# Strassen block products in the down projection of a transformer layer, with sums kept in DRAM

## The chip, the cores and the metric

The kernel runs on one core of a Trainium2 chip. The metric is the device time of one launch in microseconds. The kernel before was timed three times: 3572.49, 3582.17 and 3583.19, median 3582.17. All data is float32. A core has TensorE (PE in the profile; its weight loads PEld), VectorE (DVE), ScalarE (ACT), GpSimd (POOL) and SyncE (SP), which here issues all of the DMAs, one after another.

## The reference

One transformer layer on 2048 tokens of width 1024: modulated norm, an input projection, attention beside a gated linear recurrence, an output projection, and then the feed-forward part, where the change is.

```python
def swiglu(h, w_gu, w_down):
    a, b = jnp.split(h @ w_gu, 2, axis=-1)
    return (jax.nn.silu(a) * b) @ w_down
...
x = x + mx[2] * (jnp.concatenate([att_x, hg_x], axis=-1) @ w_out[l])
x = x + mx[5] * swiglu(modulate(rmsnorm(x, g_norm2[l]), mx[3], mx[4]), w_gu[l], w_down[l])
...
return rmsnorm(x, g_final)
```

`w_gu` is 1024x5632, `w_down` 2816x1024; 2816 is 22 blocks of 128.

## The kernel before

Every large product takes each float32 operand as a high part (rounded to the type fp32r) and a low part (what is left), and adds three matmuls: high by high, high by low, low by high. A converted tile so costs one ACT copy (the high part) and one subtraction on DVE or POOL (the low part).

**Stages.** Modulation vectors; input projection; attention and recurrence, interleaved; output projection in blocks of four token tiles of 128 (`project_token`, `mix_token`, `normed_block`, blocks 0 to 3 in turn); then the feed-forward part in two passes over halves of the tokens, pass 1 (tokens 1024 to 2047) first, then pass 0. The normed rows of blocks 2 and 3 stay in SBUF for pass 1; those of blocks 0 and 1 go through DRAM (`s_h2`).

**A pass** has three functions. `build(pair)` makes the sums T1 to T4 of the four blocks of the transposed input (DVE at L1092) and their parts (L999, L1000). `hidden(pair)` computes gate and up by Strassen's seven block products (Winograd's form): for each of the 22 blocks `ff` it loads 2 x 512 KB of `w_gu` (L1128), forms the sums S1 to S4 on POOL (L1141) and their parts (L1135, L1136), and runs seven products of 12 matmuls each (L1161) into PSUM banks A, B and C, copied and combined through tiles `r` (L1173 to L1189), giving `h` (L1189, L1195), stored to `s_hid`. `down(pair)` is a plain product: for each half `hb` of the pass's tokens, over 22 blocks `ff`, it loads 256 KB of `s_hid` (L1216) and 512 KB of `w_down` (L1218), converts both (L1221, L1222, L1225, L1226), and adds 24 matmuls (L1230) into all eight PSUM banks. After the last `ff` of a half, each of the four token tiles is finished: gate multiply (L1244), reload of the row `x1` into a single buffer (L1239) and add (L1245), squares on ACT (L1247), norm (L1249, L116, and the power on POOL at L118), scale (L1252), store (L1254). The next half's matmuls need the banks which L1244 empties.

**What sets the order.** In these stages a scheduler orders the instructions of each engine from its own estimate of the times; within a stage the tiles' buffer counts (`dw` 2, `hid` 3, `wraw` 2 for each of two tags, `tmp` 8) decide how far loads and conversions run ahead. `build(0)` is stepped through inside `down(1)` (`next(side, 0)`, every second `ff`).

Of the kernel before, what the change touches and what calls it, by code (L numbers as in the profile page):

```python
# [48 lines left out]

C_Q, C_K, C_HQ, C_I, C_FF, C_FB, C_G = 0, 512, 768, 1280, 1792, 2304, 2816  # L50
# [17 lines left out]
def block_kernel(ctx: ExitStack, tc: tile.TileContext, a: dict, out: bass.AP, dbg=None):  # L68
# [28 lines left out]
    s_hid = [dram(f"s_hid{j}", [NFF, P, 1024]) for j in range(2)]  # L97
# [468 lines left out]
    with ExitStack() as st:  # L566
# [333 lines left out]
        for item in work + [None]:  # L900
            if item is None:
# [51 lines left out]
                mix_token(0)  # L953
# [26 lines left out]
    with ExitStack() as st:  # L980
        np5 = pool(p5, "np5", 6)
        ep = pool(p5, "ep", 2)
# [22 lines left out]
        def project_token(t):  # L1005
# [7 lines left out]
            for hf in range(2):  # L1013
# [8 lines left out]
                if hf == 0 and t + 1 < NCH:  # L1022
                    mix_token(t + 1)
# [7 lines left out]
        def normed_block(blk, xns):  # L1031

            tb = blk % 2
            for k in range(KT):
# [4 lines left out]
                x = slot(vA, F32)  # L1039
# [14 lines left out]
        for blk in range(4):  # L1054
# [14 lines left out]
        tmp = pool(st, "tmp", 8, side="right")  # L1069
        wraw = pool(st, "wraw", 2, side="right")  # L1070
        hraw = pool(st, "hraw", 4, side="right")
# [42 lines left out]
        def hidden(pair):  # L1114


            with ExitStack() as d1:
# [48 lines left out]
                nxt = weights(0)  # L1166
                for ff in range(NFF):
                    nm = f"{pair}_{ff}"
                    W = nxt
                    A, B, C = (bank(f"p{n}{nm}") for n in "ABC")  # L1170
                    product(A, W["A11"], V["B11"], True, False)
                    r0 = t512(f"r0{nm}")
                    nc.scalar.activation(r0, A, AF.Copy)  # L1173
# [11 lines left out]
                    product(C, W["A12"], V["B21"], True, True)  # L1185
                    nc.vector.tensor_tensor(r0, C, r0, op=ALU.add)
                    nc.scalar.activation(r0, r0, AF.Silu)
                    h1 = t512(f"h1{nm}")
                    nc.gpsimd.tensor_tensor(h1, r1, r4, op=ALU.mult)  # L1189
                    nc.sync.dma_start(s_hid[pair][ff][:, 512:], h1)  # L1190
                    if ff + 1 < NFF:
                        nxt = weights(ff + 1)
                    product(A, W["A22"], V["T4"], False, True)
                    h0 = t512(f"h0{nm}")
                    nc.vector.tensor_tensor(h0, A, r0, op=ALU.mult)  # L1195
                    nc.sync.dma_start(s_hid[pair][ff][:, :512], h0)

        def down(pair, side):

            with ExitStack() as d2:  # L1200

                dw = pool(d2, "dw", 2)
                hid = pool(d2, "hid", 3)
                yp = pool(d2, "yp", 2)
# [6 lines left out]
                for hb in range(2):  # L1211
                    acc = [[bank(f"pd{pair}{hb}{j}{hf}") for hf in range(2)] for j in range(4)]
                    for ff in range(NFF):
# [19 lines left out]
                        if ff % 2:  # L1233
                            next(side, 0)
# [25 lines left out]
        down(1, todo)  # L1260
        for _ in todo:
            pass
        hidden(0)
        down(0, iter(()))


# [41 lines left out]
```

## Time and profile before

| | |
|---|---|
| median of three runs | 3582.17 us |
| profiled execution, its own time | 3583.7 us |
| its span (first to last instruction) | 3581.9 us, so 1.8 us lie outside |
| PE busy in the span | 3352.1 us (94 %) |
| DVE, ACT, POOL busy | 1757.0, 1549.5, 1593.0 us |
| moved by DMA | 355.97 MB, 99 GB/s in the mean |
| output projection's last matmuls | at 2114 us |
| `hidden(1)`, `down(1)` | about 2127 to 2584, 2585 to 2842 us |
| `hidden(0)`, `down(0)` | about 2866 to 3303, 3303 to 3558 us |

PE is the engine that is busy nearly all of the time, so the time is read as PE's work at the spacing of its matmuls, plus the stretches in which it idles or runs at a lower granted clock. "Idle" in a row of the trace stands in brackets, with the instruction that ended it.

### The profile page before, as it was taken

To read this page: it belongs to the slowest core of one execution; us is meant where nothing else is said; L and a number is where in the kernel's file an instruction comes from. 1 tells how busy PE (TensorE), PEld (TensorE's weight loads), DVE (VectorE), ACT (ScalarE), POOL (GpSimd) and SP (SyncE) were. 2 spreads that over 40 slices of the span, in tenths; PEclk is the share of its full clock that TensorE was granted. 3 is DMA by queue.
4 is the path that set the end of the run, shared out by engine and by line. 5 is a ranking of instruction groups with operands and counts; after the bars stand their busy time and mean duration, and the time that the engine had idled before them with its cause. 6 is when DMAs were issued, how large, how long until landed. Compare 5 with 4: busy or idle time off the path is not lost. (4 is left out here: it accounts for less than half of the span.)

```text
span 3581.9 us, 52481 instructions
## 1 busy us (share of the span) xinstructions
PE 3352.1 (94%) x19588; PEld 2793.6 (78%) x19588; DVE 1757.0 (49%) x3078; ACT 1549.5 (43%) x3167; POOL 1593.0 (44%) x1496
## 2 busy tenths in 40 slices
PE   8999999979999899999999988999999799999997
PEld 5999877968777778777777876888787678887876
DVE  6445555066667677666655474222354332222344
ACT  4322222157767567766654133333433233333232
POOL 4322232068768758768742046555201165553010
PEclk9999999989999999999999999999999899999998
DMA  7244655321121121111005432222445322222553
GB/s 231 95 140 123 176 167 167 109 85 32 36 63 34 33 69 44 31 46 40 23 24 162 159 106 74 91 76 83 150 146 171 121 92 89 73 88 85 162 173 104
DMA packets 315696, 355.97 MB, mean 99 GB/s; under 512 B 27088, under 2 KB 245168, under 8 KB 315184
## 3 DMA queue, kind: packets, MB, share of 16 engines
q1 hardware_dynamic: 315440, 352.61, 31.7%
q8 instruction: 154, 2.52, 0.3%
q14 instruction: 102, 0.84, 0.1%
HBM read 251.85 MB, written 100.68 MB: 98 GB/s over the span
## 5 line engine op out<-in xcount | busy, mean ns | idle before, releaser
L827 POOL TENSOR_TENSOR pr<-pr,fac 128x768 f32<-128x768 f32 x256 | 374.4, 1484 | 215.0 <-DMA mf<-in_k_mask_dram 101.5
L815 DVE TENSOR_REDUCE neg<-s 128x1 f32<-128x768 f32 x384 | 365.1, 954 | 199.0 <-PE s L812 198.4
L812 PE MATMUL s<-K,qs 128*128 128x512 f32 (+1 forms) x1536 | 371.5, 364 | 33.7 <-ACT pr L820 31.6
L820 ACT ACTIVATE pr<-s,neg 128x768 f32<-128x768 f32 x384 | 348.5, 908 | 73.6 <-DVE neg L819 38.1
L812 PEld LDWEIGHTS s<-K,qs 128*128 128x128 f32 x1536 | 264.0, 191 | 104.8 <-ACT pr L820 44.9
L835 PE MATMUL pt<-identr,pr 128*128 128x128 f32 x2304 | 319.8, 274 | 7.6 <-DVE oo L870 3.2
L841 ACT ACTIVATE pf<-pt 128x512 f32<-128x512 f32 x448 | 256.7, 601 | 111.4 <-PE pt L835 109.5
L1230 PE MATMUL pd<-dl,hh 128*128 128x512 f32 x704 | 277.8, 395 | 2.7 <-DVE dl L1226 2.7
L1230 PE MATMUL pd<-dh,hl 128*128 128x512 f32 x704 | 277.4, 394 | 0.0
L835 PEld LDWEIGHTS pt<-identr,pr 128*128 128x128 f32 x2304 | 261.3, 141 | 16.6 <-ACT pf L841 7.5
L848 PE MATMUL av<-pf,V 128*64 128x256 f32 x2304 | 268.7, 388 | 1.5 <-DVE pf L839 1.5
L848 PEld LDWEIGHTS av<-pf,V 128*64 128x64 f32 x2304 | 162.4, 139 | 88.3 <-issue 9.7
L1230 PE MATMUL pd<-dh,hh 128*128 128x512 f32 x704 | 181.7, 394 | 17.9 <-DVE yy L1244 14.4
L1245 POOL TENSOR_TENSOR yy<-yy,xf 128x512 f32<-128x512 f32 x24 | 30.6, 1296 | 364.6 <-DVE yy L1244 348.7
L1221 ACT ACTIVATE hh<-hr 128x512 fp32r<-128x512 f32 x88 | 55.4, 630 | 292.2 <-PE pd L1230 289.4
L1222 DVE TENSOR_TENSOR hl<-hr,hh 128x512 fp32r<-128x512 f32 x88 | 61.7, 701 | 231.7 <-ACT hh L1221 229.8
L1230 PEld LDWEIGHTS pd<-dh,hh 128*128 128x128 f32 x704 | 133.6, 190 | 48.8 <-DVE yy L1244 16.2
L635 PE MATMUL pa<-Q,M 128*128 128x128 f32 x896 | 131.4, 291 | 30.7 <-POOL Q L661 16.8
L1230 PEld LDWEIGHTS pd<-dl,hh 128*128 128x128 f32 x704 | 134.3, 191 | 31.7 <-DVE dl L1226 3.6
L1230 PEld LDWEIGHTS pd<-dh,hl 128*128 128x128 f32 x704 | 134.3, 191 | 28.2
L635 PEld LDWEIGHTS pa<-Q,M 128*128 128x128 f32 x896 | 116.4, 195 | 38.7 <-POOL Q L661 20.5
L1161 PE MATMUL pA<-x,A11h 128*128 128x512 f32 x352 | 118.9, 403 | 23.9 <-ACT A11h L1135 23.9
(290 smaller groups left out, 8698.8 us busy)
## 6 DMA issues: line engine op xcount, KB each, us to landing
w<-in_w_gu_dram SPq DMA_DIRECT2D x88, 512.0 KB
wr<-in_w_down_dram SPq DMA_DIRECT2D x88, 512.0 KB
wm<-in_w_mod_dram SPq DMA_DIRECT2D x24, 1024.0 KB
s_hid<-h SPq DMA_DIRECT2D x88, 256.0 KB
hr<-s_hid SPq DMA_DIRECT2D x88, 256.0 KB
s_q<-sq SPq DMA_DIRECT2D x128, 128.0 KB
qs<-s_q SPq DMA_DIRECT2D x32, 512.0 KB
ws<-in_w_in_dram SPq DMA_DIRECT2D x9, 1024.0 KB
```

Of the source, the lines that this page charges most:

```text
L635: nc.tensor.matmul(pa[:, cs], M[:, cs], strided(Q[:], c * P, [[2 * hs, 64 // hs], [512 + hs, 2], [1, hs]]), start=True, stop=True)
L812: nc.tensor.matmul(s[:, o:o + w], self.qs[:, hh, self.item[2], half, :], self.kv[0][:, k0 + o:k0 + o + w], start=(half == 0), stop=(half = ...
L815: nc.vector.tensor_reduce(neg[:, i:i + 1], s[:, :n], axis=AX.X, op=ALU.min)
L820: nc.scalar.activation(pr[:, k0:k0 + n], s[:, :n], AF.Exp, bias=neg[:, m:m + 1], scale=-1.0, accum_out=self.ls[:, hh, i:i + 1])
L827: nc.gpsimd.tensor_tensor(pj, pj, self.fac[:, hh, j:j + 1].to_broadcast([P, SW]), op=ALU.mult)
L835: nc.tensor.transpose(pt[:, (2 * i + hh) * P:(2 * i + hh + 1) * P], self.prs[hh][:, (2 * k2 + i) * P:(2 * k2 + i + 1) * P], ident)
L841: nc.scalar.activation(pf, pt, AF.Copy)
L848: nc.tensor.matmul(self.av[i * 64:(i + 1) * 64], self.kv[1][:, 2 * k2 + i, :], self.pf[k2][:, i * 256:(i + 1) * 256], start=(n == 0), stop ...
L1161: nc.tensor.matmul(acc, w[wi][:, k, :], x[xi][k], start=(start and k == 0 and i == 0), stop=(stop and k == KH - 1 and i == 2), skip_group_ ...
L1221: nc.scalar.activation(hh, hr, AF.Copy)
L1222: nc.vector.tensor_tensor(hl, hr, f32v(hh), op=ALU.subtract)
L1230: nc.tensor.matmul(acc[j][hf], l[:, j * P:(j + 1) * P], r[:, hf * 512:(hf + 1) * 512], start=(ff == 0 and i == 0), stop=(ff == NFF - 1 and ...
```

## The change

The down projection becomes a Strassen product too. The pass's 8 token tiles, `w_down`'s 22 rows of blocks and its 1024 columns are each cut in two, and seven block products take the place of the plain one. Each has 11 steps (`NHF`), a step having 4 token tiles x 3 matmuls: 132 matmuls a product, 924 a pass (1056 before).

- The left operands (A11, A12, A22 and the sums S1 to S4 of the hidden values) are made in `hidden`, on POOL, and stored to DRAM by their names: seven stores of 256 KB for two blocks `ff` (four before). For that `hidden` takes blocks j and j+11 in turns.
- The right operands' sums T1 to T4 of `w_down` are made once, beside `hidden(1)` (`right_sums`): 44 loads of 256 KB, 44 DVE subtractions, 44 stores to DRAM (`s_wt`). Both passes read them.
- `down` loads two times 256 KB for each step, converts each half with one ACT copy and one DVE subtraction (128x512), in two sets of tiles (`dwa`, `dwb`) used in turns.
- The eight rows tiles `y` of a pass are loaded once at its start and kept; each product's result is multiplied by the gate (DVE) and added to its rows (POOL, DVE for the last product) at the product's end. Norm and stores follow for four tiles at the sixth product's end, for the other four at the seventh's. The last two steps of the seventh product are taken token by token.
- In `hidden`, `first(ff)` draws the loading, the sums and the product A11 of the next block ahead, and the product with B21 is now the second. `tmp` has 10 buffers; `hraw` is gone.
- The output projection takes blocks 2, 3, 0, 1 in this order, so that pass 1's rows are made first. Rows of blocks 0 and 1 go through the pool `ep` on their way to DRAM (3 buffers), `np5` has 5.

```diff
-                x = slot(vA, F32)
+                x = slot(vA if blk >= 2 else ep, F32)
...
-        for blk in range(4):
+        for blk in (2, 3, 0, 1):
...
-        tmp = pool(st, "tmp", 8, side="right")
+        tmp = pool(st, "tmp", 10, side="right")
         wraw = pool(st, "wraw", 2, side="right")
-        hraw = pool(st, "hraw", 4, side="right")
...
+                def first(ff):
+                    W = weights(ff)
+                    A = bank(f"pA{pair}_{ff}")
+                    product(A, W["A11"], V["B11"], True, False)
+                    r0 = t512(f"r0{pair}_{ff}")
+                    nc.scalar.activation(r0, A, AF.Copy)
+                    return W, A, r0
+
+                def store(n, j, t):
+                    nc.sync.dma_start(s_hid[pair][n][j], t)
...
+                order = [j + half * NHF for j in range(NHF) for half in range(2)]
+                with tc.high_priority():
+                    nxt = first(order[0])
+                h = {}
+                for n, ff in enumerate(order):
+                    half, j = divmod(ff, NHF)
+                    W, A, r0 = nxt
+                    B, C = (bank(f"p{b}{nm}") for b in "BC")
+                    product(C, W["A12"], V["B21"], True, True)
+                    nc.vector.tensor_tensor(r0, C, r0, op=ALU.add)
+                    nc.scalar.activation(r0, r0, AF.Silu)
...
+                    nc.gpsimd.tensor_tensor(r1, r1, r4, op=ALU.mult)
+                    if n + 1 < NFF:
+                        nxt = first(order[n + 1])
                     product(A, W["A22"], V["T4"], False, True)
-                    h0 = t512(f"h0{nm}")
-                    nc.vector.tensor_tensor(h0, A, r0, op=ALU.mult)
-                    nc.sync.dma_start(s_hid[pair][ff][:, :512], h0)
+                    nc.vector.tensor_tensor(r0, A, r0, op=ALU.mult)
+                    h[half] = r0, r1
+                    store(("A11", "A12")[half], j, r0)
+                    if half:
+                        store("A22", j, r1)
+                        (a11, a21), (a12, a22) = h[0], h[1]
+                        s3, s2, s4 = (t512(f"s{i}{nm}") for i in "324")
+                        nc.gpsimd.tensor_tensor(s3, a11, a21, op=ALU.subtract)
+                        store("S3", j, s3)
+                        nc.gpsimd.tensor_tensor(a21, a21, a22, op=ALU.add)
+                        store("S1", j, a21)
+                        nc.gpsimd.tensor_tensor(s2, a21, a11, op=ALU.subtract)
+                        store("S2", j, s2)
+                        nc.gpsimd.tensor_tensor(s4, a12, s2, op=ALU.subtract)
+                        store("S4", j, s4)
+                        h = {}
+                        next(side, 0)
...
+        def right_sums():
+            for j in range(NHF):
+                b = {}
+                for r in range(2):
+                    for c in range(2):
+                        t = b[r, c] = tmp.tile([P, 512], F32, tag="x", name=f"wq{j}{r}{c}")
+                        nc.sync.dma_start(t, quadrant(r, c, j))
+                nc.vector.tensor_tensor(b[0, 0], b[0, 1], b[0, 0], op=ALU.subtract)
+                nc.sync.dma_start(s_wt["T1"][j], b[0, 0])
+                nc.vector.tensor_tensor(b[0, 1], b[1, 1], b[0, 1], op=ALU.subtract)
+                nc.sync.dma_start(s_wt["T3"][j], b[0, 1])
+                nc.vector.tensor_tensor(b[1, 1], b[1, 1], b[0, 0], op=ALU.subtract)
+                nc.sync.dma_start(s_wt["T2"][j], b[1, 1])
+                nc.vector.tensor_tensor(b[1, 0], b[1, 0], b[1, 1], op=ALU.subtract)
+                nc.sync.dma_start(s_wt["T4"][j], b[1, 0])
+                yield
...
         def down(pair, side):
+                dwa = pool(d2, "dwa", 4)
+                y0p = pool(d2, "y0p", 4)
+                dwb = pool(d2, "dwb", 4)
+                y1p = pool(d2, "y1p", 4)
...
+                direct = {"B11": (0, 0), "B21": (1, 0), "B22": (1, 1)}
+                step = [0]
+                def load(ln, rn, j):
+                    n = step[0]
+                    step[0] += 1
+                    raw = wraw.tile([P, D], F32, tag=f"w{n % 2}", name=f"lr{pair}_{n}")
+                    nc.sync.dma_start(raw[:, :512], s_hid[pair][ln][j])
+                    nc.sync.dma_start(raw[:, 512:], quadrant(*direct[rn], j) if rn in direct else s_wt[rn][j])
+                    out = []
+                    for i in range(2):
+                        src = raw[:, i * 512:(i + 1) * 512]
+                        hi, lo = ((dwa, dwb)[n % 2].tile([P, 512], F32R, tag="p", name=f"{x}{pair}_{n}{i}")
+                                  for x in ("dh", "dl"))
+                        nc.scalar.activation(hi, src, AF.Copy)
+                        nc.vector.tensor_tensor(lo, src, f32v(hi), op=ALU.subtract)
+                        out.append((hi, lo))
+                    return out
...
+                def add(acc, tb, cb, t, eng):
+                    cs = slice(cb * 512, (cb + 1) * 512)
+                    x = tmp.tile([P, 512], F32, tag="x", name=f"yg{pair}{tb}{cb}{t}_{step[0]}")
+                    nc.vector.tensor_tensor(x, acc, gate2[:, cs], op=ALU.mult)
+                    eng.tensor_tensor(ys[tb, t][:, cs], ys[tb, t][:, cs], x, op=ALU.add)
...
+                plan = [("A11", "B11", "A", 1, 0, (0, 0)), ("S1", "T1", "B", 1, 0, (1, 1)),
+                        ("S2", "T2", "A", 0, 0, (0, 1)), ("S4", "B22", "B", 0, 1, (0, 1)),
+                        ("S3", "T3", "A", 0, 0, (1, 1)), ("A12", "B21", "C", 1, 1, (0, 0)),
+                        ("A22", "T4", "A", 0, 1, (1, 0))]
+                for n, (ln, rn, bk, start, stop, (tb, cb)) in enumerate(plan):
...
+                    def mms(t, j, f):
+                        (lh, ll), (rh, rl) = f
+                        for i, (l, r) in enumerate(((lh, rh), (lh, rl), (ll, rh))):
+                            nc.tensor.matmul(cur[t], l[:, t * P:(t + 1) * P], r,
+                                             start=bool(start and j == 0 and i == 0),
+                                             stop=bool(stop and j == NHF - 1 and i == 2), skip_group_check=True)
+                    kept = []
+                    for j in range(NHF):
+                        f = load(ln, rn, j)
+                        if n == 0 and j == 1:
+                            rows(0)
+                            rows(1)
+                        if last and j >= NHF - 2:
+                            kept.append((j, f))
+                            continue
+                        for t in range(4):
+                            mms(t, j, f)
+                        if step[0] % 7 == 0:
                             next(side, 0)
+                    for t in range(4):
+                        for j, f in kept:
+                            mms(t, j, f)
+                        add(cur[t], tb, cb, t, nc.vector if last else nc.gpsimd)
+                        if n == 3 or n == 5:
+                            square(0, 1 if n == 3 else 0, t)
+                        if n == 4:
+                            square(1, 1, t)
+                            nc.gpsimd.tensor_tensor(ys[1, t][:, 512:], ys[1, t][:, 512:], gfin[:, 512:], op=ALU.mult)
+                        if n == 5:
+                            rs = norm(0, t)
+                            nc.vector.scalar_tensor_tensor(ys[0, t], ys[0, t], rs, gfin, op0=ALU.mult, op1=ALU.mult)
+                            nc.sync.dma_start(out[0, row(0, t), :], ys[0, t])
+                        if n == 6:
+                            square(1, 0, t)
+                            rs = norm(1, t)
+                            y = ys[1, t]
+                            nc.vector.scalar_tensor_tensor(y[:, :512], y[:, :512], rs, gfin[:, :512],
                                                            op0=ALU.mult, op1=ALU.mult)
+                            nc.scalar.activation(y[:, 512:], y[:, 512:], AF.Copy, scale=rs)
+                            nc.sync.dma_start(out[0, row(1, t), :], y)
...
-        hidden(1)
+        hidden(1, right_sums())
         todo = build(0)
         down(1, todo)
         for _ in todo:
             pass
-        hidden(0)
+        hidden(0, iter(()))
         down(0, iter(()))
```

PE executes 1848 matmuls of the down projection instead of 2112; the number of those of `hidden` (3696) and of all stages before is as it was. Three places show what moved.

First SP's queue, where `hidden(0)` ends and `down(0)` begins. Before (`hr`, `wr` are the loads of `down`, `xf` the first row that is reloaded, the numbers behind them the step):

```order
1087 L1218 DMA wr_3_31403<-in_w_down_dram 128x1024
1088 L1196 DMA s_hid_86<-h_19_31013 128x512
1089 L1190 DMA s_hid_86<-h_20_31102 128x512
1090 L1196 DMA s_hid_86<-h_20_31157 128x512
1091 L1190 DMA s_hid_86<-h_21_31246 128x512
1092 L1208 DMA gate_31281<-s_mod 128x1024
1093 L1210 DMA gfin_31283<-in_g_final_dram 128x1024
1094 L1196 DMA s_hid_86<-h_21_31261 128x512
1095 L1239 DMA xf_32085<-s_x_83 128x1024
1096 L1216 DMA hr_4_31437<-s_hid_86 128x512
```

And now (`lr` is the load of a step, `y` the rows kept):

```order
1317 L1179 DMA s_hid0A_87<-r_21_31718 128x512
1318 L1179 DMA s_hid0S_90<-s_21_31822 128x512
1319 L1289 DMA y_31893<-s_x_83 128x1024
1320 L1289 DMA y_31895<-s_x_83 128x1024
1321 L1179 DMA s_hid0S_92<-s_21_31823 128x512
1322 L1289 DMA y_31897<-s_x_83 128x1024
1323 L1289 DMA y_31899<-s_x_83 128x1024
1324 L1289 DMA y_31901<-s_x_83 128x1024
1325 L1289 DMA y_31903<-s_x_83 128x1024
1326 L1289 DMA y_31905<-s_x_83 128x1024
1327 L1271 DMA lr_5_31988<-s_hid0A_86 128x512
1328 L1272 DMA lr_5_31988<-in_w_down_dram 128x512
```

The load of step 4 stood behind the last store and one row's load; now step 5's stands behind the last stores and all eight rows' loads, and step 6's, not shown, just ahead of this piece.

Next DVE at the end of `down(0)`. Before, the last two token tiles (`yy` is the row tile, `pd` the PSUM bank):

```order
2806 L1244 TENSOR_TENSOR yy_32997<-pd_32163,gate_31281 128x512
2807 L1244 TENSOR_TENSOR yy_32997<-pd_32164,gate_31281 128x512
2808 L1252 SCALAR_TENSOR_TENSOR yy_32979<-yy_32979,rs_xf_32991,gfin_31283 128x1024
2809 L1245 TENSOR_TENSOR yy_32997<-yy_32997,xf_32995 128x512 x2
2810 L1249 TENSOR_TENSOR ss1f_33005<-ssf_32998 128x1
2811 L116 TENSOR_SCALAR ms_xf_33007<-ss1f_33005 128x1
2812 L1244 TENSOR_TENSOR yy_33015<-pd_32165,gate_31281 128x512
2813 L1244 TENSOR_TENSOR yy_33015<-pd_32166,gate_31281 128x512
2814 L1252 SCALAR_TENSOR_TENSOR yy_32997<-yy_32997,rs_xf_33009,gfin_31283 128x1024
2815 L1245 TENSOR_TENSOR yy_33015<-yy_33015,xf_33013 128x512 x2
2816 L1249 TENSOR_TENSOR ss1f_33023<-ssf_33016 128x1
```

And now, the last three (`y` the row tile, `yg` the bank times the gate):

```order
3007 L1310 TENSOR_TENSOR ss1f_33799<-ssf_33212 128x1
3008 L1297 TENSOR_TENSOR y_31903<-y_31903,yg_77_33814 128x512
3009 L121 TENSOR_SCALAR ms_xf_33801<-ss1f_33799 128x1
3010 L1296 TENSOR_TENSOR yg_77_33834<-pd0A_31856,gate_31849 128x512
3011 L1365 SCALAR_TENSOR_TENSOR y_31901<-y_31901,rs_xf_33803,gfin_31851 128x512
3012 L1310 TENSOR_TENSOR ss1f_33819<-ssf_33219 128x1
3013 L1297 TENSOR_TENSOR y_31905<-y_31905,yg_77_33834 128x512
3014 L121 TENSOR_SCALAR ms_xf_33821<-ss1f_33819 128x1
3015 L1365 SCALAR_TENSOR_TENSOR y_31903<-y_31903,rs_xf_33823,gfin_31851 128x512
3016 L1310 TENSOR_TENSOR ss1f_33839<-ssf_33226 128x1
3017 L121 TENSOR_SCALAR ms_xf_33841<-ss1f_33839 128x1
3018 L1365 SCALAR_TENSOR_TENSOR y_31905<-y_31905,rs_xf_33843,gfin_31851 128x512
```

Multiply, add, norm and scale of the four tiles are now woven into each other, with no load of a row among them, and each tile has half a row (512 columns) here: the first half of the columns of these four tiles is the last to be ready, the other half has its multiply by `gfin` from POOL after the fifth product and its scale by the norm from ACT.

Last DVE inside `down(1)`, where the second product has ended, at step 22. Before, a stretch with as much of `build(0)` in it (L1092, the sums):

```order
2346 L1092 TENSOR_TENSOR x_26521<-x_26257,x_26241 128x512
2347 L1092 TENSOR_TENSOR x_26523<-x_26259,x_26243 128x512
2348 L1092 TENSOR_TENSOR x_26525<-x_26261,x_26245 128x512
2349 L1092 TENSOR_TENSOR x_26527<-x_26263,x_26247 128x512
2350 L1222 TENSOR_TENSOR hl_0_26174<-hr_0_26169,hh_0_26173 128x512
2351 L1226 TENSOR_TENSOR dl_0_26178<-wr_0_26171,dh_0_26177 128x1024
2352 L1092 TENSOR_TENSOR x_26617<-x_26265,x_26521 128x512
2353 L1222 TENSOR_TENSOR hl_1_26210<-hr_1_26205,hh_1_26209 128x512
```

And now (L1096 is the same line of `build`, `dl` the low parts of a step):

```order
2435 L1279 TENSOR_TENSOR dl_220_27038<-lr_22_27034,dh_220_27037 128x512
2436 L1279 TENSOR_TENSOR dl_221_27042<-lr_22_27034,dh_221_27041 128x512
2437 L1296 TENSOR_TENSOR yg_22_27022<-pd1B_26733,gate_26412 128x512
2438 L1296 TENSOR_TENSOR yg_22_27025<-pd1B_26734,gate_26412 128x512
2439 L1296 TENSOR_TENSOR yg_22_27028<-pd1B_26735,gate_26412 128x512
2440 L1296 TENSOR_TENSOR yg_22_27031<-pd1B_26736,gate_26412 128x512
2441 L1096 TENSOR_TENSOR x_27172<-x_26613,x_26597 128x512
2442 L1096 TENSOR_TENSOR x_27174<-x_26615,x_26599 128x512
2443 L1096 TENSOR_TENSOR x_27176<-x_26617,x_26601 128x512
2444 L1096 TENSOR_TENSOR x_27178<-x_26619,x_26603 128x512
2445 L1279 TENSOR_TENSOR dl_230_27061<-lr_23_27057,dh_230_27060 128x512
2446 L1279 TENSOR_TENSOR dl_231_27065<-lr_23_27057,dh_231_27064 128x512
```

Between the low parts of step 22 and those of step 23 there are now eight operations in a row, four at the product's end and four of `build(0)`.

105 lines of the change are left out of this document (37 added, 68 removed).

## The prediction

> **What bounds the kernel.** I read the busy totals first, then the matmul groups of the down projection, then PE's timeline for its spacing and idle gaps, then windows around the gaps, last the chain of waits at the end.
>
> ```profile
> PE 3352.1 (94%) x19588; PEld 2793.6 (78%) x19588; DVE 1757.0 (49%) x3078; ACT 1549.5 (43%) x3167; POOL 1593.0 (44%) x1496
> L1230 PE MATMUL pd<-dl,hh 128*128 128x512 f32 x704 | 277.8, 395 | 2.7 <-DVE dl L1226 2.7
> L1230 PE MATMUL pd<-dh,hl 128*128 128x512 f32 x704 | 277.4, 394 | 0.0
> L1230 PE MATMUL pd<-dh,hh 128*128 128x512 f32 x704 | 181.7, 394 | 17.9 <-DVE yy L1244 14.4
> ...
> 3462.37 0.39 PE L1230 MATMUL pd<-dh,hl 128*128 128x512 f32 x1
> ...
> 3463.73 0.39 PE L1230 MATMUL pd<-dh,hl 128*128 128x512 f32 x1
> ...
> 3450.00:3550.00 100.00, 100.00 (x443) 82.80 (x442) 38.25 (x42) 29.91 (x40) 0.55 (x1) 1.00 0.43 134
> 2400.00:2500.00 100.00, 100.00 (x429) 80.39 (x428) 27.19 (x43) 36.04 (x63) 53.30 (x40) 1.00 0.27 85
> ```
>
> PE is busy 94 % of the span. The down projection has 3 x 704 = 2112 matmuls. A single one takes 0.39 us, but they overlap, so the mean of a group is no price: the two rows of the timeline are six starts apart, (3463.73 - 3462.37)/6 = 0.2267 us each. The window of `down` agrees: 100/0.2267 = 441, and 443 are in it with those cut at its edges. The window of the hidden products, by the same two fewer, gives 100/427 = 0.2342, say 0.2343. What is left beside this work are gaps. Windows give, in this order: length, busy us and count of PE, PEld, DVE, ACT, POOL, then the granted clock, the DMA share and GB/s.
>
> ```profile
> 2719.92 0.79 PE L1230 MATMUL pd<-dh,hh 128*128 128x512 f32 x1 [5.14 <-DVE yy L1244]
> 2700.00:2740.00 40.00, 31.45 (x122) 24.71 (x121) 20.31 (x32) 13.14 (x26) 12.76 (x12) 0.87 0.55 179
> 3430.00:3460.00 30.00, 21.86 (x80) 16.80 (x79) 14.76 (x21) 8.75 (x18) 9.21 (x10) 0.89 0.63 214
> 2575.00:2605.00 30.00, 25.55 (x102) 19.79 (x101) 24.34 (x37) 18.31 (x30) 1.29 (x1) 0.94 0.49 165
> 3295.00:3325.00 30.00, 28.46 (x123) 22.70 (x122) 11.10 (x14) 9.95 (x14) 1.29 (x1) 1.00 0.54 193
> 2841.49 0.39 PE L1230 MATMUL pd<-dh,hl 128*128 128x512 f32 x1
> 2865.76 1.22 PE L1161 MATMUL pA<-x,A11h 128*128 128x512 f32 x2 [23.88 <-ACT A11h L1135]
> 2161.22 1.22 PE L1161 MATMUL pA<-x,S2h 128*128 128x512 f32 x2 [12.10 <-ACT r L1173]
> 3558.02 0.39 PE L1230 MATMUL pd<-dh,hl 128*128 128x512 f32 x1
> 3570.33 3.50 DMA xf<-s_x
> ```
>
> A gap costs its idle time and the lower clock behind it, so I take a window less its matmuls at full spacing. The changes of token half lose 40 - 122 x 0.2267 = 12.3 us in pass 1 and 30 - 80 x 0.2267 = 11.9 in pass 0; entering `down` loses 30 - 102 x 0.2267 = 6.9 and 30 - 123 x 0.23 = 1.7. From `down(1)` to `hidden(0)` PE idles 23.9 us, and behind the last matmul (3558.4) the span goes on for 23.5 us, of which each token waits 3.5 us for its row's reload.
>
> **The change, part by part**, against the profiled execution (3583.7 us, of which 1.8 lie outside the span; the median of the runs shown is 1.5 lower).
>
> *1. Fewer matmuls.* 2112 - 1848 = 264 fewer at 0.2267: **-59.8**. Should the new operands run at the hidden products' 0.2343, each of 1848 costs 0.0076 more, +14.0. I keep 0.2267: the converted tiles of both operands again lie in `down`'s own pools.
>
> *2. Change of token half.* It goes: **-24.2**. What comes in its place is term 7.
>
> *3. Tail.* The rows are in SBUF. These are the durations of the last 28 us:
>
> ```profile
> L1245 DVE TENSOR_TENSOR yy<-yy,xf 128x512 f32<-128x512 f32 x8 | 5.2, 686 | 2.9 <-DMA xf<-s_x 2.9
> L1247 ACT ACTIVATE xf<-yy 128x512 f32<-128x512 f32 x8 | 5.0, 624 | 22.3 <-DVE yy L1245 22.3
> L118 POOL TENSOR_TENSOR rs_xf<-ms_xf,mhalf 128x1 f32<-128x1 f32 x4 | 2.2, 548 | 121.6 <-DVE ms_xf L116 121.6
> ...
> 3577.49 0.75 DVE yy L1252
> ```
>
> The tokens' last matmuls end 6 x 0.2267 = 1.36 us apart. I lay DVE's new order (multiply 0.69, add 0.69, sum 0.16, mean 0.15, scale 0.75; squares 0.62 and their 0.19 on ACT; power 0.55 on POOL) behind them: the fourth token's scale ends about 7.5 us after the last matmul; before, from the last scale's start at 3577.49 plus 0.75 x 2 to the end were 2.9. With 0.6 for hops that is 11 instead of 23.5: **-12.5** (-9 to -14).
>
> *4. `down(1)` to `hidden(0)`.* The first ACT conversion still stands behind the last token's norm, now at about 8 us instead of 23.9; the lower clock behind the gap stays: **-16** (-10 to -19).
>
> *5. Start of `hidden(1)`.* A11 and A12 need none of the T sums, so 24 matmuls run ahead of them. But POOL has the sums of two blocks ahead of its low parts of T, and S2, which ended the 12.1 us gap, comes only about 7 us earlier when I lay its order out with their mean of 1.29 us (term 8's rows), while one product (12 matmuls, 2.8 us) less is done ahead of it: **-4.5** (-12 to +8).
>
> *6. Entering `down`.* Eight rows' loads (8 x 0.52 = 4.2 MB), which wait for `hidden`'s tiles to come free, stand on SP ahead of step 5's load. The fastest stretch of the trace moved 328 GB/s:
>
> ```profile
> 20.00:40.00 20.00, 19.10 (x103) 10.28 (x101) 13.94 (x46) 5.50 (x7) 1.11 (x2) 0.94 0.98 328
> ```
>
> The rows with 1.6 MB of stores and 0.5 MB of the step take 19 us; the five steps before it feed PE for 5 x 2.72 = 13.6. With conversion a stall of 8 us, and a lower clock behind it, say 13.5 in pass 1 and 10 in pass 0, less 6.9 and 1.7: **+15** (0 to +35).
>
> *7. The bursts at the products' ends.* A step is 12 x 0.2267 = 2.72 us of PE. Its conversion:
>
> ```profile
> L1221 ACT ACTIVATE hh<-hr 128x512 fp32r<-128x512 f32 x88 | 55.4, 630 | 292.2 <-PE pd L1230 289.4
> L1222 DVE TENSOR_TENSOR hl<-hr,hh 128x512 fp32r<-128x512 f32 x88 | 61.7, 701 | 231.7 <-ACT hh L1221 229.8
> L1092 DVE TENSOR_TENSOR x<-x,x 128x512 f32<-128x512 f32 x16 | 21.2, 1351 | 0.0
> L1092 DVE TENSOR_TENSOR x<-x,x 128x512 f32<-128x512 f32 x6 | 3.8, 677 | 0.0
> ```
>
> Two ACT copies and two DVE parts a step are 1.26 and 1.40 us, hence half of each engine. A step's tiles come free when the step two before it ends, and the chain (0.63 + 0.63 + 0.70 and hops, about 2.05) then has some 1.3 us to spare beyond one step. A burst beyond that stalls PE: four multiplies (2.8 us) at each product's end, and in `down(1)` four to six operations of `build(0)` beside them; POOL's adds also stretch DVE's two-operand work: the last two rows are one line beside a busy POOL (2110 to 2180) and with POOL idle (2600 to 2700), 1.351 against 0.677 us. I take **+14** in pass 1 and **+4** in pass 0, that is +18 (0 to +45).
>
> The Trainium skill, page "SBUF — State Buffer", section "Who interferes with whom", says that a DVE instruction with two SBUF inputs and a GpSimd instruction that reads SBUF exclude each other. Those two rows agree. By it each burst of four POOL adds could hold the low parts back by up to their whole length.
>
> *8. More beside the hidden products.* Seven stores instead of four, four more POOL sums for two blocks, and in pass 1 the 44 loads, differences and stores of `right_sums`.
>
> ```profile
> L1189 POOL TENSOR_TENSOR h<-r,r 128x512 f32<-128x512 f32 x20 | 32.6, 1632 | 35.7 <-DVE r L1184 33.4 <-issue 2.3
> L1136 POOL TENSOR_TENSOR A22l<-w,A22h 128x512 fp32r<-128x512 f32 x19 | 24.5, 1292 | 8.1 <-ACT A22h L1135 8.1
> L1141 POOL TENSOR_TENSOR S<-w 128x512 f32<-128x512 f32 x17 | 22.0, 1292 | 1.3
> ```
>
> For two blocks PE works 168 x 0.2343 = 39.4 us; POOL has 2 x (1.63 + 7 x 1.29) = 21.3 us now and 4 x 1.29 = 5.2 more, 67 %. DMA in pass 1 is 5.9 MB in 39.4 us, 150 GB/s, below half of 328. I cost it at **0** (0 to +25): the next block's weights are converted about 20 us ahead of need, and that covers a wait. Unseen is the case in which the ten `tmp` tiles come free too late.
>
> The Trainium skill, page "DMA: Bandwidth & Descriptors", section "Bandwidth", speaks against the change: transfers should be batched to 1 MiB or more for three quarters of the peak, and these are 256 KB. By it a step's 0.5 MB could take longer than its 2.72 us. The trace is milder: 134 GB/s kept the DMA engines at 0.43 with half of the loads at 256 KB.
>
> The new output order and `ep` I take at 0 (-3 to +3): the same matmuls, beside the same loads.
>
> Sum: -59.8 - 24.2 - 12.5 - 16 - 4.5 + 15 + 18 + 0 = -84.0, so 3583.7 - 84.0 = 3499.7, on the medians' scale about **3500**.
>
> **Rivals.**
> *A: the conversion sets the step.* For: each set of tiles serves one step, and beside POOL a DVE part takes 1.35 us, not 0.70. Against: half-idle engines. There are 154 steps; 0.28 us more for each is +43: **3543**. *B: the DMAs arrive late*, the entry stalls at their upper end and products begin dry, as each load waits on SP behind the one before: +20 beyond term 6 and +12, the middle of term 8: **3532**. *C, the slower side: SP's queue in `hidden(1)`.* A store waits for its POOL sum, `wq` loads wait behind it for tiles, DVE's difference waits for those loads with the hidden products' copies behind it, and the next weights' load stands behind all this on SP. If this ring is longer than two blocks' 39.4 us, PE waits in each of 11 rounds. It outweighs the gain from 84/11 = 7.6 us a round; at 10 us the time is **3610**. For: POOL's 67 % and the full order of the ring; against: about 20 us of lead. *D: only the matmuls go*, the waits saved being given back entirely: -60, **3524**; with the spacing of 0.2343 as well, **3538**.
>
> **How the numbers follow.** Forecast 0.60; A 0.13; B 0.12; C 0.07; D 0.08. A change of this kernel is told from none at about 0.3 %, 11 us. A, B and D are faster by more than that, but for part of A (steps 0.5 us longer, 154 x 0.5 = 77, take nearly all of the gain), 0.03. So faster 0.89, same 0.04, slower 0.07. The range takes A's and B's times in and the forecast's own spread: the favourable ends of terms 5 to 7 would give 3470, seldom all; from 3472 to 3550.
>
> **What would show it.** Right: 1848 matmuls of `down` spaced 0.2267; no gap with the release by L1244's successor; a tail of 11 us behind the last matmul; the gap before `hidden(0)` near 8 us; a stall of about 8 us about 14 us into each `down`. Wrong: `hidden` windows with fewer than 428 matmuls in 100 us (C); many gaps of 0.5 us and more inside the products that end with a DVE low part (A) or a load (B).

## The result, and the profile after

| | before | changed |
|---|---|---|
| median | 3582.68 us (4 runs, 3572.49 to 3584.04) | 3532.49 us (4 runs, 3526.94 to 3535.76) |
| ratio | | 0.9864, 95 % interval 0.9842 to 0.9887 |
| profiled execution, span | 3581.9 us | 3525.1 us |
| output projection's last matmul ends | 2114.3 | 2102.9 |
| from there to the end | 1467.6 | 1422.2 |
| behind the last matmul of `down(0)` | 23.5 | 13.5 |

The changed kernel is 50 us faster, 1.4 %; forecast were 82. The two profiled executions are 57 us apart, but 11.4 of that lie ahead of the feed-forward part, where the change only takes the output blocks in another order. In the profiled executions of all the runs below, this point lies anywhere from 2100.7 to 2119.0 us with the old order and from 2102.9 to 2113.5 with the new one, so those 11.4 are not told from chance. I count from there: -45.4 us, against a forecast of -84 that lay wholly behind that point.

PE's timeline of the changed kernel shows the idle time (in brackets, with what ended it) in four places: at the start of `hidden(1)`, at the entry of each `down`, at the products' ends in `down(1)`, and before `hidden(0)`.

```profile
2129.87 1.12 PE L1042 MATMUL nt<-identr,xn 128*128 128x128 f32 x4 [17.69 <-DVE x L1045]
2155.15 1.22 PE L1165 MATMUL pA<-x,S2h 128*128 128x512 f32 x2 [9.09 <-ACT r L1175]
...
2608.42 2.07 PE L1331 MATMUL pd1A<-dh,dh 128*128 128x512 f32 x4 [7.50 <-ACT dh L1278]
2666.69 0.79 PE L1331 MATMUL pd1A<-dl,dh 128*128 128x512 f32 x1 [4.43 <-DVE dl L1279]
2702.45 0.79 PE L1331 MATMUL pd1B<-dl,dh 128*128 128x512 f32 x1 [3.23 <-DVE dl L1279]
...
2846.14 1.22 PE L1165 MATMUL pA<-x,A11h 128*128 128x512 f32 x2 [11.45 <-ACT A11h L1139]
...
3304.60 2.08 PE L1331 MATMUL pd0A<-dh,dh 128*128 128x512 f32 x4 [4.52 <-ACT dh L1278]
```

The first row is new: the last four transposes of the output projection wait 17.7 us for DVE, and all the hidden products stand behind them on PE. What DVE and POOL did meanwhile, by groups (line, engine, operation, tiles, count, busy us, mean ns), from 2110 to 2128 us:

```profile
L1096 DVE TENSOR_TENSOR x<-x,x 128x512 f32<-128x512 f32 x10 | 15.4, 1604 | 0.0
L1140 DVE TENSOR_TENSOR S2l<-S,S2h 128x512 fp32r<-128x512 f32 x1 | 1.8, 1751 | 0.0
...
L1140 POOL TENSOR_TENSOR S1l<-S,S1h 128x512 fp32r<-128x512 f32 x2 | 3.4, 1712 | 0.0
L1145 POOL TENSOR_TENSOR S<-w,S 128x512 f32<-128x512 f32 x2 | 3.4, 1706 | 0.0
```

Ten T sums run on DVE ahead of the eviction (L1045), each 1.6 us long instead of 0.68, beside POOL operations that take 1.71 instead of 1.29.

The windows of the changed kernel at the two entries, the rest of both `down`s, and the hidden products (columns as in the prediction):

```profile
2580.00:2615.00 35.00, 22.73 (x78) 17.43 (x79) 17.72 (x22) 8.91 (x16) 6.45 (x4) 0.80 0.87 308
3280.00:3325.00 45.00, 37.37 (x139) 29.70 (x140) 20.76 (x28) 13.45 (x24) 7.69 (x6) 0.85 0.71 246
2610.00:2834.30 224.30, 206.79 (x861) 166.58 (x860) 154.00 (x214) 99.99 (x184) 45.46 (x32) 0.95 0.56 179
3325.00:3511.60 186.60, 181.09 (x787) 146.40 (x785) 123.63 (x165) 81.90 (x152) 43.79 (x31) 1.00 0.58 185
2300.00:2500.00 200.00, 200.00 (x858) 160.63 (x858) 76.08 (x102) 73.16 (x124) 137.03 (x102) 1.00 0.48 158
```

Read as before, a window less its count at 0.2267 us: the entries lose 17.3 and 13.5 us, the rest of `down(1)` 29.1 and of `down(0)` 8.2. (The first and the third window share the 5 us from 2610 to 2615, with 16 matmuls, which lose 1.4 us.) The hidden products run on undisturbed, although POOL is at 69 % and DMA at 158 GB/s: 856 in 200 us before, 858 now.

### The profile page after: what moved, and what is told of

It is laid out like the page before. It is cut to its first block, busy times and chain, and to the rows that moved or that the text cites. A ratio compares the mean times of both kernels' runs of the same rounds, so it can differ in the third digit from the quotient of the medians.

```text
span 3525.1 us, 53153 instructions
## 1 busy us (share of the span) xinstructions
PE 3291.1 (93%) x19324; PEld 2737.8 (78%) x19324; DVE 1909.1 (54%) x3274; ACT 1599.6 (45%) x3307; POOL 1780.2 (51%) x1616
## 5 line engine op out<-in xcount | busy, mean ns | idle before, releaser
L1279 DVE TENSOR_TENSOR dl<-lr,dh 128x512 fp32r<-128x512 f32 x308 | 239.6, 818 | 163.9 <-ACT dh L1278 163.9
L1278 ACT ACTIVATE dh<-lr 128x512 fp32r<-128x512 f32 x308 | 178.3, 623 | 247.3 <-PE pd0A L1331 73.4
L1297 POOL TENSOR_TENSOR y<-y,yg 128x512 f32<-128x512 f32 x48 | 72.0, 1514 | 335.5 <-DVE yg L1296 331.7
L640 PE MATMUL pa<-Q,M 128*128 128x128 f32 x896 | 130.3, 289 | 30.7 <-POOL Q L666 16.9
L640 PEld LDWEIGHTS pa<-Q,M 128*128 128x128 f32 x896 | 115.2, 193 | 38.6 <-POOL Q L666 20.5
L1140 POOL TENSOR_TENSOR S1l<-S,S1h 128x512 fp32r<-128x512 f32 x44 | 59.1, 1343 | 139.6 <-ACT S1h L1139 136.7
L345 PE MATMUL f<-hTh,wh 128*128 128x512 f32 (+1 forms) x320 | 121.0, 378 | 6.3 <-ACT ft L374 6.3
L1165 PE MATMUL pA<-x,A11h 128*128 128x512 f32 x352 | 113.5, 404 | 11.5 <-ACT A11h L1139 11.5
L1165 PE MATMUL pA<-x,S2h 128*128 128x512 f32 x352 | 112.2, 400 | 9.1 <-ACT r L1175 9.1
L345 PE MATMUL f<-hTh,wl 128*128 128x512 f32 (+1 forms) x320 | 119.2, 372 | 0.0
L345 PE MATMUL f<-hTl,wh 128*128 128x512 f32 (+1 forms) x320 | 119.0, 372 | 0.0
L123 POOL TENSOR_TENSOR rs_x<-ms_x,mhalf 128x1 f32<-128x1 f32 x34 | 20.3, 602 | 187.3 <-DVE ms_x L121 187.2
```

What stands on the lines that cost most here:

```text
L345: nc.tensor.matmul(pm[:, :n], w[wi][:, k, c0:c0 + P], hT[b][hi][:, k, :], start=(k == 0 and i == 0), stop=(k == KT - 1 and i == 2))
L640: nc.tensor.matmul(pa[:, cs], M[:, cs], strided(Q[:], c * P, [[2 * hs, 64 // hs], [512 + hs, 2], [1, hs]]), start=True, stop=True)
L1165: nc.tensor.matmul(acc, w[wi][:, k, :], x[xi][k], start=(start and k == 0 and i == 0), stop=(stop and k == KH - 1 and i == 2), skip_group_ ...
L1278: nc.scalar.activation(hi, src, AF.Copy)
L1279: nc.vector.tensor_tensor(lo, src, f32v(hi), op=ALU.subtract)
```

## The experiments

All are the changed kernel with the edit shown, unless it says otherwise. "Feed-forward" is the time from the output projection's last matmul to the end of the profiled execution.

| run | median us | ratio to before (95 %) | feed-forward us |
|---|---|---|---|
| changed kernel | 3532.49 | 0.9864 (0.9842 to 0.9887) | 1422.2 |
| plain_order | 3522.38 | 0.9840 (0.9822 to 0.9857) | 1411.5 |
| diff_late | 3501.63 | 0.9781 (0.9763 to 0.9799) | 1389.0 |
| rows_gated | 3514.73 | 0.9815 (0.9794 to 0.9836) | 1402.1 |
| no_add | 3516.10 | 0.9825 (0.9804 to 0.9846) | 1399.9 |
| pad32 | 3510.20 | 0.9803 (0.9786 to 0.9820) | 1395.5 |
| side_after | 3530.57 | 0.9867 (0.9848 to 0.9886) | 1421.4 |
| combo | 3480.94 | 0.9725 (0.9708 to 0.9741) | 1367.8 |
| combo_dve | 3468.89 | 0.9691 (0.9676 to 0.9705) | 1359.2 |
| combo_pool | 3472.84 | 0.9702 (0.9687 to 0.9716) | 1360.0 |
| pad160 (one run) | 3529.74 | | 1417.3 |
| before_pad (kernel before) | 3579.02 | 0.9992 (0.9978 to 1.0006) | 1462.6 |
| before_pad160 (kernel before) | 3547.70 | 0.9920 (0.9903 to 0.9936) | 1439.7 |

The kernel before, timed beside each group of these runs, had medians from 3578.4 to 3582.7 us; differences of under about 4 us between two rows mean nothing.

### The start of `hidden(1)`: plain_order and diff_late

```diff
-        for blk in (2, 3, 0, 1):
+        for blk in range(4):
...
-                x = slot(vA if blk >= 2 else ep, F32)
+                x = slot(vA, F32)
```

(with `mix_token`'s order and the buffer counts of `np5` and `ep` as before.)

> The output projection goes back to blocks 0, 1, 2, 3 with its old pools; all else as changed. In the changed kernel the last four transposes wait 17.7 us behind DVE's T sums, and 39 us are lost between the last output matmul and 2190 us (28 before). Theory (the new block order puts T sums ahead of the evictions): that wait goes, the loss falls to 28 or below, 10 to 16 us faster than the changed kernel, about 3517 to 3522. Rival (the wait comes from hidden's new start, which draws more weights' sums ahead): within 3 us of the changed kernel's 3532.

Measured: 3522.4, 10 us faster. The 17.7 us wait is gone, since DVE evicts first:

```profile
2110.56 2.96 DVE L1045 TENSOR_SCALAR x<-nt,modc 128x512 f32<-128x512 f32 x4
```

For the start's loss I count the hidden matmuls in the 87 us behind the last output matmul: 226 before, 178 in the changed kernel, 217 here, each at its kernel's spacing, beside 5.6 us of transposes. Before that is 87 - 226 x 0.2342 - 5.6 = 28.5 us; the changed kernel loses 39.9 and plain_order 30.7. So the new order of the blocks, with its buffers, cost 9 us. The start is still 2 us worse than before, not better as expected: that `first` draws two products ahead of the T sums saved nothing that shows.

The other edit keeps the new order and holds the T sums back until the last eviction:

```diff
+                if blk == 1 and k == KT - 1:
+                    nc.scalar.activation(mark, x[:, 0:1], AF.Copy)
...
                 t = slot(tmp, F32)
+                if pair:
+                    nc.scalar.activation(t[:, 0:1], mark, AF.Copy)
```

> The new block order is kept; the T sums of pass 1 wait for the last eviction by a one-column copy that marks it. Theory (evictions queued behind T sums): no idle time of more than 5 us ahead of the last transposes, the first 24 hidden matmuls run at once, 5 to 12 us faster than 3532. Rival (all of the sums and parts on DVE and POOL are the bound, in whatever order): the idle time only moves to the product with S1 or S2, within 3 us of 3532.

Measured: 31 us faster, far more than either theory allowed. The wait of the transposes fell from 17.7 to 6.5 us, but a new one of 15.2 us came at the product with A12:

```profile
2127.53 1.12 PE L1042 MATMUL nt<-identr,xn 128*128 128x128 f32 x4 [6.54 <-DVE x L1045]
2161.65 1.22 PE L1170 MATMUL pC<-x,A12h 128*128 128x512 f32 x2 [15.16 <-ACT A12h L1144]
```

So most of the wait only moved, and the start's loss fell from 39.9 to 35.1 us (204 matmuls at 0.2268). That is 5 us. Of the rest, 24 lie where nothing was edited, in the hidden products: 884 of them in 200 us instead of 858. The tile `mark` had moved the tiles behind it by 32 bytes. This needed runs of its own.

### The spacing of the hidden products: pad32, before_pad, before_pad160, pad160

```diff
         sm = pool(st, "smf", 4, side="right")
+        pad = sm.tile([P, 8], F32, tag="pad", name="pad", bufs=1)
+        nc.gpsimd.memset(pad, 0.0)
```

> The changed kernel with one 32-byte tile (per partition) more at the base of the right side of SBUF, set to zero once and used by nothing. It moves the moving operands of the hidden products from addresses that are 32 modulo 64 to multiples of 64, as the marker tile of diff_late did unasked. Theory (the address sets the spacing): the hidden windows have 884 matmuls in 200 us instead of 859, 0.2267 us instead of 0.2333; 3696 x 0.0066 = 24 us faster than the changed kernel, about 3508. Rival (diff_late's order of the sums gave its 31 us): 859, and within 3 us of 3532.

> The kernel before with the same 32-byte tile and nothing else. Theory (addresses): hidden windows of 884 in 200 us instead of 856, 3696 x 0.0076 = 28 us faster than before, ratio 0.992. Rival (something in the changed kernel, its DMA or its order, is needed too): 856, ratio 1.00.

Measured: pad32 gains 22 us and its hidden products run at the spacing of `down`. The same tile in the kernel before gains nothing (ratio 0.9992): its windows have 859. A multiple of 64 is not the rule, then. I looked up, in the built programs, the addresses of both operands of these matmuls (the one of 512 columns is called moving, the one of 128 columns, which PEld loads, stationary), and chose the next two sizes by them (160 bytes, `[P, 40]`).

> The kernel before with an unused tile of 160 bytes a partition, so that the hidden products' moving operands lie at 320 modulo 512 bytes, where those of pad32 and diff_late lie (before: 480; before_pad, which gained nothing: 448; the changed kernel: 352); the stationary ones stay at 64. Theory (moving and stationary offsets alike modulo 256 give 0.2267 us): hidden windows of 884 in 200 us, 3696 x 0.0075 = 28 us faster than before, ratio 0.992. Rival (the changed kernel's own order of matmuls is needed too): below 870, ratio above 0.997.

> The changed kernel with the same 160 bytes, which put the moving operands at 192 modulo 512, 128 off the stationary ones as in before_pad. Theory (alike modulo 256): about 860 in 200 us, 0.2325. Rivals: a multiple of 64 is enough in the changed kernel, or alike modulo 128: 884.

Measured: both as the theory said, though pad160 is a single run. The windows of the hidden products, first before, then before_pad160, pad32 and pad160:

```profile
2300.00:2500.00 200.00, 200.00 (x856) 160.80 (x855) 53.51 (x83) 72.09 (x124) 106.58 (x80) 1.00 0.27 84
```

```profile
2300.00:2500.00 200.00, 200.00 (x884) 165.62 (x883) 54.23 (x84) 74.24 (x127) 110.39 (x83) 1.00 0.28 87
```

```profile
2300.00:2500.00 200.00, 200.00 (x884) 165.62 (x883) 81.69 (x104) 74.70 (x127) 142.29 (x106) 1.00 0.49 158
```

```profile
2300.00:2500.00 200.00, 200.00 (x862) 162.17 (x861) 76.98 (x102) 72.31 (x122) 139.21 (x103) 1.00 0.47 152
```

| moving operand's offset modulo 512 bytes (the stationary one's is 64 in all of these) | in 200 us | runs |
|---|---|---|
| 480 | 856 | before |
| 448 | 859 | before_pad |
| 352 | 858 | changed kernel |
| 192 | 862 | pad160 |
| 320 | 884 | diff_late, pad32, before_pad160, combo |
| 64 | 443 in 100 us, that is 0.2267 each | `down` before |

The kernel before varies the stationary operand, too. In its input projection (L340) the moving operand lies at 64 throughout, the stationary one at 64 or at 480, by the buffer that its tile got. At 64 the matmuls follow each other every 0.2267 us (43 starts from 597.60 to 607.12 us), at 480 every 0.2333 us (45 starts from 121.57 to 131.83 us). So a moving operand in a fast place is not enough; the stationary one's place counts as well.

### The entry of `down`: rows_gated

```diff
-                        if n == 0 and j == 1:
-                            rows(0)
-                            rows(1)
+                        if step[0] in (3, 5, 7, 9, 11, 13, 15, 17):
+                            one_row((step[0] - 3) // 2, f[1][1])
```

(`one_row` copies one column of a step's low part into the row tile, and only then loads it.)

> The eight rows of a pass are loaded one at a time, every second step from step 2 on (a one-column copy from a step's low part holds each load back); before, all eight stood ahead of step 5's load. Theory (those loads delay step 5): the idle times of 7.5 us at 2608 and 4.5 us at 3305 go, with the lower clock behind them 12 to 18 us faster than 3532. Rival (DMA has too little to spare, whatever the order): the same time is lost later in the first product, within 4 us of 3532.

Measured: 18 us faster; `down(1)`, counted to the first product of `hidden(0)`, goes from 272.1 to 262.8 us and `down(0)` from 237.6 to 228.2. Both waits are gone, and the first product shows no other in their place. The windows of the two entries, now 35 - 122 x 0.2267 = 7.3 and 45 - 175 x 0.2267 = 5.3 us lost, of 17.3 and 13.5:

```profile
2590.00:2625.00 35.00, 30.69 (x122) 24.54 (x123) 21.29 (x27) 12.24 (x22) 8.17 (x9) 0.90 0.85 293
3280.00:3325.00 45.00, 41.69 (x175) 33.64 (x175) 27.31 (x35) 17.07 (x30) 14.27 (x15) 0.96 0.72 245
```

The order on SP was the cause; DMA, at 293 GB/s there, carried the same bytes. In the changed kernel, with all eight rows in a row, the DMA engines were busy without a break from 2585 to 2610 us (a share of 1.03, 371 GB/s), and step 5's load stood behind that.

### The products' ends: no_add and side_after

```diff
-                    eng.tensor_tensor(ys[tb, t][:, cs], ys[tb, t][:, cs], x, op=ALU.add)
+                    if eng is nc.vector:
+                        eng.tensor_tensor(ys[tb, t][:, cs], ys[tb, t][:, cs], x, op=ALU.add)
```

> Leaves out POOL's adds to the rows after the first six products, so the sums in the output are incomplete. In the changed kernel the products' ends lose 33 us in pass 1 and 8 in pass 0 against matmuls at 0.2267 us. Theory (DVE's work with two SBUF operands waits beside POOL's adds: 1.3 to 1.8 us instead of 0.68): DVE's T sums in down(1) take 0.7 us, the loss falls to below 20 and 4, 12 to 20 us faster than 3532. Rival (it is the number of DVE operations in the burst): 33 falls by less than 5, 0 to 6 us faster.

```diff
-                        if step[0] % 7 == 0:
+                        if False:
                             next(side, 0)
```

> build(0), the T sums and parts of pass 0, is taken out of down(1) and stands behind it. Theory (its DVE operations beside the products' ends are why pass 1 loses 33 us at them and pass 0 8): down(1) gets 15 to 25 us shorter, from 272 to 247 to 257; its 28 sums and 32 parts then stand ahead of hidden(0), whose start is 15 to 35 us later, so the total is 3525 to 3550. Rival (the four gate multiplies and POOL's adds alone): down(1) stays above 265.

Measured: no_add is 16 us faster (22 in the feed-forward part of its profiled execution), side_after the same as the changed kernel (its saving stands behind `down(1)` as a wait of 26.5 us instead of 11.5 before `hidden(0)`). Their windows of `down(1)`, first no_add, then side_after:

```profile
2613.80:2824.60 210.80, 199.81 (x858) 162.84 (x858) 133.65 (x214) 98.45 (x184) 9.52 (x8) 0.98 0.58 190
```

```profile
2611.00:2813.70 202.70, 197.19 (x857) 159.91 (x856) 132.01 (x178) 88.83 (x164) 45.09 (x32) 1.00 0.61 196
```

At 0.2267 us a matmul they lose 16.3 and 8.4 us, the changed kernel 29.1. So it takes both parts of the pile to lose so much: without `build(0)` pass 1 loses what pass 0 loses; without POOL's adds 13 us less, though `build(0)` is all there. In pass 0, which has no `build(0)`, no_add loses 2.0 us instead of 8.2 (178.1 us with 777 matmuls). From 2600 to 2800 us the mean T sum takes 0.82 us in no_add and 1.12 in the changed kernel, the mean low part 0.69 and 0.78. The burst after step 22, from 2655 to 2666 us in the changed kernel, shows both:

```profile
L1096 DVE TENSOR_TENSOR x<-x,x 128x512 f32<-128x512 f32 x4 | 5.4, 1416 | 0.0
L1279 DVE TENSOR_TENSOR dl<-lr,dh 128x512 fp32r<-128x512 f32 x4 | 2.6, 684 | 1.4 <-ACT dh L1278 1.4
L1296 DVE TENSOR_TENSOR yg<-pd1B,gate 128x512 f32<-128x512 f32 x4 | 2.5, 681 | 0.0
```

The multiplies, which read PSUM, take 0.68 us beside POOL's adds. The four T sums, which read SBUF twice, take 1.42 in the same stretch. Eight operations that I had priced at 5.5 us so take 7.9, with the next step's low parts behind them.

### Putting it together: combo, combo_dve, combo_pool

> The three edits together: the old order of the output blocks, the rows loaded one at a time, and the 32-byte tile. Theory (three separate causes): their gains add, -10 - 17 - 24 = -51 from the changed kernel's 3532, about 3480. Rival (one gives back what another saves): above 3492.

combo is plain_order, rows_gated and pad32 in one. Measured 3480.9, 52 us faster than the changed kernel: the three add (10, 18 and 22). On top of it, two ways to thin the bursts:

```diff
-                        add(cur[t], tb, cb, t, nc.vector if last else nc.gpsimd)
+                        add(cur[t], tb, cb, t, nc.vector)
```

> combo, with the adds to the rows on DVE instead of POOL. Theory (POOL's adds cost DVE more beside them than they are worth): T sums in down(1) near 0.7 us, each product's end 2.8 us more of DVE work in the burst; down(1) from 263 to 255 to 260 and down(0) from 226 to 224, 3 to 10 us faster than combo's 3481. Rival (the length of the burst is what counts): 0 to 10 us slower.

```diff
-                nc.vector.tensor_tensor(t, x, y, op=ALU.subtract)
+                (nc.vector if pair else nc.gpsimd).tensor_tensor(t, x, y, op=ALU.subtract)
```

(and the low parts in `build(0)` on POOL.)

> combo, with build(0)'s sums and low parts on POOL instead of DVE: 16 sums and 28 parts at 1.3 us are 57 us of POOL in down(1)'s 250. Theory (bursts in DVE's queue stall PE): down(1)'s 263 falls by 10 to 18, towards the 239 that it had without build(0) plus what POOL's reads cost, 3463 to 3471. Rival (the port that DVE and POOL share: more POOL work slows every low part of a step to 1.3 us, 2.6 a step): 263 or more, 3481 or slower.

Measured: combo_dve 12 us faster than combo, combo_pool 8. In combo_dve `down(1)` takes 254.4 us instead of 262.7, with more work on DVE. In combo_pool it takes 253.0, and the total lies just above the theory's range. The mean low part of a step there is 1.12 us long, and while POOL is busy PE waits for it in one step after the other:

```profile
L1281 DVE TENSOR_TENSOR dl<-lr,dh 128x512 fp32r<-128x512 f32 x130 | 138.4, 1116 | 36.7 <-ACT dh L1280 33.4 <-issue 3.4
...
2637.14 0.50 PE L1333 MATMUL pd1A<-dl,dh 128*128 128x512 f32 x1 [0.39 <-DVE dl L1281]
2640.54 0.50 PE L1333 MATMUL pd1A<-dl,dh 128*128 128x512 f32 x1 [0.39 <-DVE dl L1281]
2643.94 0.50 PE L1333 MATMUL pd1A<-dl,dh 128*128 128x512 f32 x1 [0.39 <-DVE dl L1281]
```

These rows are 3.40 us apart, a step of 2.72 us and 0.68 more. So the port's rival was right about the slowing, and PE does pay for it, in some 15 of the 77 steps. Its 263 did not come since the piles went in exchange: the steps of 6.8 to 9.1 us that combo has behind the entry are at most 4.4 us long here. **combo_dve, 3468.9 us, beats both kernels: 3.1 % under before**, and 2.2 % under before_pad160, the kernel before with the fast spacing.

## Why the prediction was right and wrong

The time lies in the stated range and the sign was right, but the gain is made up otherwise than forecast. By the prediction's own terms, in the feed-forward part of the profiled executions:

| term | forecast | measured |
|---|---|---|
| 1 fewer matmuls | -59.8 | -59.8 at an unchanged 0.2267; hidden spacing 0.2342 to 0.2333, -3.3 more |
| 2 change of token half | -24.2 | -24.2 |
| 3 tail | -12.5 | -10.0 |
| 4 before `hidden(0)` (idle) | -16 | -12.4 (23.9 to 11.5) |
| 5 start of `hidden(1)` | -4.5 | +11.4 (28.5 to 39.9) |
| 6 entries | +15 | +22.2 (17.3 + 13.5 - 8.6) |
| 7 bursts | +18 | +35.9 (29.1 - 1.4 counted in term 6, + 8.2) |
| 8 beside the hidden products | 0 | 0 |
| sum | -84 | -40, of -45.4 |

The terms are read from places of their own and come 5 us short of the whole. So 38.6 us of the forecast gain were missed, and two terms make most of that.

Right was term 1, the matmuls. The waits that were to go (terms 2 to 4) did go, 46.6 us of 52.7. But the new waits (terms 5 to 7) cost 69.5 us instead of 28.5, more than the removed ones gave. The forecast had waits add 24 us to the matmuls' gain; measured, they took some 18 of it away (59.8 and 3.3 less 45.4). By its mechanism the result is so nearest to rival D, all saved waits given back, which had a chance of 0.08. That the time still fell into the range is owed to the range's width.

**Term 7 was mis-sized**, 18 us. The mechanism was named (a burst longer than the spare time of the double buffer) and the Trainium skill's rule with it. I had shown that a T sum takes 1.351 us beside POOL, and still priced the burst by its count. The Trainium skill's page "SBUF — State Buffer", section "Who interferes with whom", has a DVE instruction with two SBUF inputs contend with a GpSimd instruction that reads SBUF, under a lock that only one of them holds. no_add and combo_dve agree (the mean T sum from 2600 to 2800 us falls from 1.12 to 0.82 and 0.75 us), down to the gate multiplies with one SBUF operand, which kept their 0.68. The turns were not quite whole, though: alone a low part lasts 0.68 us and a POOL operation 1.29, together 1.97, and in combo_pool such a pair follows the one before every 1.70.

**Term 5 failed in its mechanism**, 16 us. "A11 and A12 need none of the T sums, so 24 matmuls run ahead of them" is true of data and false of queues: on PE these matmuls stand behind the last transposes, those wait for evictions, and the evictions stood behind T sums on DVE. With it fell "the new output order and `ep` I take at 0": plain_order puts 9 us of the 16 there. It could have been seen in the order of DVE's instructions, which is fixed before the run.

Term 6 had the right cause, shown by rows_gated, and was 7 us small. In terms 3 and 4 I laid DVE's order too tightly. The changed kernel's last matmul and last scale:

```profile
3511.23 0.39 PE L1331 MATMUL pd0A<-dh,dl 128*128 128x512 f32 x1
...
3520.23 0.75 DVE L1365 SCALAR_TENSOR_TENSOR y<-y,rs_xf,gfin 128x512 f32<-128x512 f32 x1 [0.73 <-POOL rs_xf L123]
```

The scale ends 9.4 us behind the last matmul, not 7.5, since each power on POOL waits for a mean that DVE reaches late, and 4.1 us, not 2.9, follow it. Term 8 held: hidden's extra sums and stores are hidden wholly. Of the other rivals, C is refuted by the window of the hidden products. B did not happen as put: the entries cost 7 us more than term 6, not 20, and the hidden products nothing; that the time falls on B's 3532 is chance. A did not happen as put either: 58 of the 76 intervals between the steps of `down(1)` are at most 2.8 us long, and the longer ones lie at the entry and at bursts.

## What to carry to other kernels

Work that "runs ahead" must be followed through every in-order queue that it stands in, not through its data alone. Side work on DVE cost nothing here under the steady stream of the hidden products (term 8), and cost PE dearly where it piled up ahead of a double buffer with little time to spare; beside POOL its operations took 1.4 to 1.8 us instead of 0.68. Waits that a change removes are to be weighed against those that it makes: here the new ones were the larger. And when a small edit gains far more than its theory allows, look for what it moved in memory.

## What the runs showed of the hardware that was not expected

The same 128x512 fp32r matmul follows the one before at 0.2267 us or at 0.2326 to 0.2342 us, by where its two operands begin in a partition. With the stationary operand at 64 modulo 512 bytes, the fast places of the moving one were 64 and 320, the slow ones 192, 352, 448 and 480; with the moving operand at 64 and the stationary one at 480 the spacing was slow as well, 0.2333. That fits operands whose offsets agree modulo 256. It also fits a rule by which both must lie at 64 modulo 256; no run here separates the two. An unused tile of 160 bytes makes the kernel before 0.8 % faster (ratio 0.9920, 0.9903 to 0.9936), while the whole change made it 1.4 % faster.
